# A decoder layer with an expert lookup: small tensors of gathered tokens by way of DRAM, transposes later, 96 gathered tokens instead of 88

## The chip, the core and the metric

The kernel runs on one core of a Trainium2 chip. The metric is the device time of one execution in microseconds (us). A profiled execution has a span (first to last instruction in the trace) and its own time, which also holds what lies around the span.

## What is computed

The input is 256 tokens of width 1024. The layer normalizes them, projects them, mixes them by linear attention in four heads and by block-sparse attention in eight, projects back and adds the input. Then comes the expert lookup, and that is where the change is:

```python
q = (xt @ w_query).reshape(T, 8, 2, 128)
s = einsum('thpk', q, subkeys)               # 8 heads, 2 halves, 128 sub-keys
sv, si = top_k(s, 16)                        # per half
cand = sv[:, :, 0, :, None] + sv[:, :, 1, None, :]
top_s, pos = top_k(cand, 16)                 # 16 of 256 candidates per head
expert = take(si[..., 0] * 128 + si[..., 1], pos);  gate = softmax(top_s)
act = gelu(einsum('thkd,td->thk', u_tab[expert], xt))
out = einsum('thk,thkd->td', gate * act, v_tab[expert])
```

Each token takes 8 x 16 = 128 of 16384 experts. The tables u and v hold 16384 rows of 1024 floats, 64 MB each.

## The kernel before

The tokens of the lookup are divided. For the first NS tokens the kernel gathers the 128 rows of u and of v that each needs. For the other ND = 256 - NS it multiplies with the whole of both tables and lets a grid of gates, zero where an expert was not chosen, pick the right ones.

**Dense part.** The tables pass through SBUF in tiles of 512 KB, 128 for u and 128 for v. SyncE's queue (SP) loads them in order into a ring of 14 buffers, the next load at every `take`. In the u stage (`for jp in range(64)`) each of the 128 tiles takes eight matmuls of 128x128 by ND columns (line 120); ScalarE applies the gelu (line 840). In the v stage each tile takes eight more (line 881), which add into three PSUM banks. At the end of the v stage DVE adds these to `x2d`, the residual (line 898), in three pieces, and they go out (line 899).

**Before the tables: the q stage.** 16 weight tiles for the queries are each divided into a high and a low part, by ScalarE (line 100) and DVE (line 101), and multiplied in three passes (lines 69 to 71); products with the sub-keys follow, each 128 columns wide (line 725). Between them DVE finds the 16 largest values; the rest of this search is a list `work[0]` for the first 128 tokens, worked off in the first nine pairs of tiles of the u stage, and a list `work[1]` for the other 128, spread up to pair `J0`. Its results (two index arrays `ij`, line 640, and the gates) are transposed on TensorE (`turn`, line 645, and `turn_gates`, line 684), spread by ScalarE (lines 647, 689), and from pair 31 on one-hot arrays and a grid of gates are made of them, four tokens at a time (lines 797 to 817).

**Gathered part.** I call one token's share of one table a "few". GpSimd (POOL) gathers the 128 rows of its experts in one indirect DMA of 512 KB into one of five buffers `rowsof` (line 743). For u, DVE multiplies the rows with the token's normalized row and sums along each row (line 751); for v, DVE multiplies each row by its gate times activation and adds to a running sum (lines 761, 763). `few_to` issues them evenly over both stages; they run u first, then v. The tokens share buffers by layout: FEW lists (first token, number of tokens n, parts m). In a layout, partitions are m blocks of n tokens, and block b handles slots b*128/m and up of each token. Then one column of indices names 128 rows and one DVE instruction handles them. `ys` holds a layout's n rows m times over (2, 8 and 16 blocks), `rs` their scales, `ixs` the expert numbers and `gs` the gates. ScalarE issues a DMA for each block and each of these four: `rows_of_few` (lines 568, 569) and `parts_of` (line 654), 4 x 26 = 104. At the end matmuls with the 0/1 matrix `sums` add the parts (line 892), DVE adds the residual (line 893), and the rows go out (line 894).

**What sets the order.** Each engine executes its instructions in one fixed order. The order in the program is set by a scheduler when the kernel is built: it simulates a timeline and hands each engine its instructions as they become ready there. Buffers and data dependencies turn into semaphore waits; an instruction that waits holds everything behind it on its engine.

Of the kernel before, what the change touches and what calls it, by code (L numbers as in the profile page):

```python
# [9 lines left out]
F32 = mybir.dt.float32  # L10
# [5 lines left out]
OP = mybir.AluOpType  # L16
AX = mybir.AxisListType

D = 1024
# [4 lines left out]
GS = 2.0 ** 14  # L24
NEXP = 128
J0 = 31
NS = 88
FEW = ((0, 64, 2), (64, 16, 8), (80, 8, 16))
ND = S - NS
SLOTS = 128  # L30
OFF = {"gq": 0, "gk": 256, "gv": 512, "gg": 1024, "gr": 1536, "mq": 1552, "mk": 2064, "mv": 2576}
# [4 lines left out]
def layer(ctx: ExitStack, tc: tile.TileContext, a):  # L36
    nc = tc.nc
    ve, sc_, pe, gp = nc.vector, nc.scalar, nc.tensor, nc.gpsimd
# [6 lines left out]
    keep = ctx.enter_context(tc.tile_pool(name="keep", bufs=1))  # L45

    def bank(tag):
        return psum.tile([128, 512], F32, name=tag, tag=tag, bufs=4 if tag == "sc" else 2)
# [3 lines left out]
    p = bank("mm")  # L52
# [158 lines left out]
    rows = {}  # L211
# [268 lines left out]
    x2T = mid.tile([128, NC, S], F32, name="x2T")  # L480
# [24 lines left out]
    act_p = ctx.enter_context(tc.tile_pool(name="actA", bufs=1))  # L505
# [6 lines left out]

    ixs = keep.tile([128, NS], U32, name="ixs")
    gs = keep.tile([128, NS], F32, name="gs")
    hs = keep.tile([128, NS], F32, name="hs")
    rs = keep.tile([128, 3], F32, name="rs")

    sums = act_p.tile([128, len(FEW), NS], F32, name="sums")
    gp.memset(sums, 0.0)
    for l, (t0, n, m) in enumerate(FEW):  # L520
        o = sums[:, l, t0:t0 + n]
# [3 lines left out]
    tk = tk_ctx.enter_context(tc.tile_pool(name="tk", bufs=1))  # L525
# [8 lines left out]
    rstd2 = tk.tile([128, NT], F32, name="rstd2")  # L534
    ss2 = tk.tile([128, NT, 2], F32, name="ss2")
    yf = wide.tile([128, NC, ND], F32, name="yf", tag="xhi")
    ys2 = wide.tile([128, 2, D], F32, name="ys", tag="xlo")
    ys = [ys2[:, 0], ys2[:, 1], act_p.tile([128, D], F32, name="ys3")]
    spillT = nc.dram_tensor("x2_cols", (128, NC, ND), F32, kind="Internal").ap()
    rows_x2 = nc.dram_tensor("x2_rows", (NS, D), F32, kind="Internal").ap()  # L540

    def x2_rows(tt):
        x2 = tk.tile([128, D], F32, name="x2")
        for hf in range(2):
            p = bank("tr")
            for c in range(4):
                pe.transpose(p[:, c * 128:(c + 1) * 128], x2T[:, 4 * hf + c, tt * 128:(tt + 1) * 128], ident)
            ve.tensor_copy(x2[:, hf * 512:(hf + 1) * 512], p)
            junk = tk.tile([128, 512], BF, name="junk", tag="junk")
            sc_.activation(junk, x2[:, hf * 512:(hf + 1) * 512], AF.Square, accum_out=ss2[:, tt, hf:hf + 1])  # L550
        if tt == 0:
            nc.scalar.dma_start(rows_x2, x2[0:NS])
        gp.tensor_tensor(rstd2[:, tt:tt + 1], ss2[:, tt, 0:1], ss2[:, tt, 1:2], op=OP.add)

    def norm2():
        nc.scalar.dma_start(spillT, x2T[:, :, NS:])
        rstd_of(rstd2, D, NT)
        row = as_row(tk, rstd2, "rrow2")
        for c in range(NC):
            ve.scalar_tensor_tensor(yf[:, c], x2T[:, c, NS:], n2[:, c:c + 1], row[:, NS:], op0=OP.mult, op1=OP.mult)  # L560

    def rows_of_few():

        n2b = tk.tile([128, D], F32, name="x2")
        nc.scalar.dma_start(n2b, a["n2b"])
        for l, (t0, n, m) in enumerate(FEW):
            for b in range(m):
                nc.scalar.dma_start(ys[l][b * n:(b + 1) * n], rows_x2[t0:t0 + n])  # L568
                nc.scalar.dma_start(rs[b * n:(b + 1) * n, l:l + 1], rstd2[t0:t0 + n, 0:1])  # L569
            ve.scalar_tensor_tensor(ys[l], ys[l], rs[:, l:l + 1], n2b, op0=OP.mult, op1=OP.mult)  # L570


    scs = [tk.tile([128, NT, 4, 128], F32, name=f"scs{b4}") for b4 in range(4)]
# [4 lines left out]
    ij = tk.tile([128, 2, NT, 8, 16], F16, name="ij")  # L578
    cands = [tk.tile([128, 8, 112], F32, name="cand") for _ in range(NT)]
    later = []  # L580

    def top16(vals, idx, src):
        ve.max(vals[:, 0:8], src)
# [51 lines left out]
    def slots3(tt, w, eq):  # L635
        n = 8
        while n > 1:
            ve.tensor_tensor(eq[:, :, 0:n], eq[:, :, 0:n], eq[:, :, n:2 * n], op=OP.add)
            n //= 2
        ve.tensor_tensor(ij[:, w, tt], eq[:, :, 0], eq[:, :, 1], op=OP.add)  # L640
        later.append(lambda: turn(tt, w))

    def turn(tt, w):
        p = bank("tr").bitcast(F16)
        pe.transpose(p[:, :128], ij[:, w, tt].rearrange("p h k -> p (h k)"), identh)
        src, ts = many(tt, p)
        sc_.copy(idxT[:, w, ts], src[:, :, None].to_broadcast([128, ts.stop - ts.start, 2]))

    def parts_of(dst, src):

        for t0, n, m in FEW:
            w = SLOTS // m
            for b in range(m):
                nc.scalar.dma_start(dst[b * n:(b + 1) * n, t0:t0 + w], src[t0:t0 + n, b * w:(b + 1) * w])  # L654

    def experts():

        num = tk.tile([128, SLOTS], U32, name="num")
        r, c = (ij[:, w, 0].rearrange("p h k -> p (h k)") for w in range(2))
        numf = tk.tile([128, SLOTS], F32, name="numf")  # L660
        ve.scalar_tensor_tensor(numf, c, 128.0, r, op0=OP.mult, op1=OP.add)
        ve.tensor_copy(num, numf)
        parts_of(ixs, num)

    def gates(tt):
        gt = top[:, tt]
# [5 lines left out]
    def gates2(tt):  # L672
        gt = top[:, tt]
        sm = tk.tile([128, 8], F32, name="sm")
        ve.tensor_reduce(sm, gt, AX.X, OP.add)
        ve.reciprocal(sm, sm)
        ve.tensor_tensor(gt, gt, sm[:, :, None].to_broadcast([128, 8, 16]), op=OP.mult)
        if tt == 0:
            parts_of(gs, gt.rearrange("p h k -> p (h k)"))
        later.append(lambda: turn_gates(tt))  # L680

    def turn_gates(tt):
        p = bank("tr")
        pe.transpose(p[:, :128], top[:, tt].rearrange("p h k -> p (h k)"), ident)

        src, ts = many(tt, p)
        full = tk.tile([128, 128], F32, name="full")[:, :ts.stop - ts.start]
        g16 = tk.tile([128, 128], F16, name="g16")[:, :ts.stop - ts.start]
        sc_.activation(full, src, AF.Copy, scale=GS)
        sc_.copy(g16, full)  # L690
        sc_.copy(gf[:, 0, ts], g16)
        ve.tensor_tensor(gf[:, 1, ts], full, g16, op=OP.subtract)


    work = [[(1.6, lambda b=b, tt=tt: top16(sv[:, tt, b], si[:, tt, b], scs[b // 4][:, tt, b % 4])) for b in range(16)]
            for tt in range(NT)]
# [48 lines left out]

    place = [l for l, (_, n, _) in enumerate(FEW) for _ in range(n)]

# [73 lines left out]
    left1 = sum(c for c, _ in work[1])  # L821
    all1, spent = left1, 0.0
    for jp in range(64):
        pv = bank("mm")[:, :2 * ND].rearrange("p (k t) -> p k t", k=2)
        turns, later = later, []
        for k in range(2):
            by_col_whole(pv[:, k], take(("u", jp), k), yf)
        for f in turns:
            f()
        if jp == J0:  # L830
            assert not work[1] and not later
            tk_ctx.close()
            actB_p = ctx.enter_context(tc.tile_pool(name="actB", bufs=1))
            act[1] = actB_p.tile([128, 64, ND], F32, name="actB")
            oh = ctx.enter_context(tc.tile_pool(name="oh", bufs=2))
            one_hots(0)
        o = act_at(2 * jp, 2 * jp + 2)
        T = 4 * done_q
        if T < ND:
            sc_.activation(o[:, :, T:], pv[:, :, T:], AF.Gelu)  # L840
        if T:
            gl = oh.tile([128, 2, ND], F32, name="gl", bufs=1)
            sc_.activation(gl[:, :, :T], pv[:, :, :T], AF.Gelu)
            ve.tensor_tensor(o[:, :, :T], o[:, :, :T], gl[:, :, :T], op=OP.mult)
        if work[0]:
            spent -= 4.8
            while work[0] and spent < 0:
                c, f = work[0].pop(0)
                spent += c
                f()  # L850
            j1 = jp + 1
        else:
            few_to((jp - j1 + 1) * 2 * NS // (64 - j1 + 61))
            while work[1] and all1 - left1 < all1 * (jp + 1 - j1) / (J0 - 1 - j1):
                c, f = work[1].pop(0)
                left1 -= c
                f()
        while jp > J0 and done_q < NQ and done_q * (62 - J0) < (jp - J0) * NQ:
            grid_group(done_q, 2 * jp + 2)
            done_q += 1  # L860
            if done_q % 2 == 1 and done_q + 1 < NQ:
                one_hots(done_q + 1)
# [3 lines left out]
    for _ in range(3):  # L866
        p = bank("sc")[:, :3 * ND]
# [6 lines left out]
    for jp in range(64):  # L874
# [13 lines left out]
        if jp == 62:  # L888
            for hf in range(2):
                fs = slice(hf * 512, (hf + 1) * 512)  # L890
                for l in range(len(FEW)):
                    pe.matmul(end[hf][0:NS], sums[:, l], ys[l][:, fs], start=l == 0, stop=l == len(FEW) - 1)  # L892
# [76 lines left out]
```

## Time and profile before

| | |
|---|---|
| three runs | 874.48, 874.9, 876.65 us |
| median | 874.9 us |
| profiled execution, own time | 877.12 us |
| its span | 875.3 us |
| TensorE matmuls (PE) | 823.0 us busy (94%) |
| TensorE weight loads (PEld) | 777.0 us (89%) |
| DVE | 482.1 us (55%) |
| ScalarE (ACT) | 247.3 us (28%) |
| GpSimd (POOL) | 215.1 us (25%) |
| DMA | 261.67 MB, 299 GB/s on average |

The table rows of u and v that are streamed and those that are gathered account for nearly all of the DMA bytes: 162.87 MB went through SP's queue and 92.29 MB through GpSimd's. Busy shares are averages over stages that differ; a matmul that has been issued and is being fed counts as busy. A record of line 881 or 120 is one matmul of 168 columns.

### The profile page before, as it was taken

To read this page: it belongs to the slowest core of one execution; us is meant where nothing else is said; L and a number is where in the kernel's file an instruction comes from. 1 tells how busy PE (TensorE), PEld (TensorE's weight loads), DVE (VectorE), ACT (ScalarE), POOL (GpSimd) and SP (SyncE) were. 2 spreads that over 40 slices of the span, in tenths; PEclk is the share of its full clock that TensorE was granted. 3 is DMA by queue.
4 is the path that set the end of the run, shared out by engine and by line. 5 is a ranking of instruction groups with operands and counts; after the bars stand their busy time and mean duration, and the time that the engine had idled before them with its cause. 6 is when DMAs were issued, how large, how long until landed. Compare 5 with 4: busy or idle time off the path is not lost.

```text
span 875.3 us, 14841 instructions
## 1 busy us (share of the span) xinstructions
PE 823.0 (94%) x5734; PEld 777.0 (89%) x5734; DVE 482.1 (55%) x1060; ACT 247.3 (28%) x660; POOL 215.1 (25%) x252
## 2 busy tenths in 40 slices
PE   9999999928997499999999999999999999999995
PEld 6876689828997399999999999999999999999993
DVE  4795367494899644446666777645455445410003
ACT  5556345403220211019677776200000000000000
POOL 4141103000001833323222232433333333300000
PEclk9997899967999699999999999999999999999998
DMA  9453027814976899999999999999999999999701
GB/s 340 167 167 121 25 79 229 248 45 139 328 236 222 301 403 409 408 409 408 400 339 360 367 352 382 349 408 408 409 409 408 409 408 409 409 409 354 234 2 48
DMA packets 75551, 261.67 MB, mean 299 GB/s; under 512 B 10433, under 2 KB 12497, under 8 KB 75353
## 3 DMA queue, kind: packets, MB, share of 16 engines
q1 hardware_dynamic: 44883, 162.87, 50.0%
q0 software_dynamic: 25344, 92.29, 27.4%
q10 hardware_dynamic: 5254, 5.57, 2.3%
q8 instruction: 45, 0.74, 0.3%
q14 instruction: 25, 0.20, 0.1%
HBM read 258.50 MB, written 2.10 MB: 298 GB/s over the span
## 4 chain that ended last, share of the span: by engine, by line
PE 82%; DVE 7%; DMA 5%; ACTq 3%; ACT 1%; issue 1%; POOL 1%; SPq 0%; DVEq 0%
PE sc L881 31%; PE mm L120 28%; PE mm L71 4%; PE mm L69 4%; PE mm L70 4%; DMA raw<-in_v_rows 2%; PE tr L808 2%; ACTq L654 1%; PE sc L388 1%; ACTq L569 1%; PE mm L892 1%; ACTq L568 1%; DMA xT<-in_xT 1%; DMA ixs<-num 1%; PE sc L369 1%
## 5 line engine op out<-in xcount | busy, mean ns | idle before, releaser
L120 PE MATMUL mm<-yf,raw 128*128 128x168 f32 x1184 | 175.8, 307 | 0.0
L120 PEld LDWEIGHTS mm<-yf,raw 128*128 128x128 f32 x1184 | 169.5, 190 | 0.4 <-DMA raw<-in_u 0.4
L761 DVE SCALAR_TENSOR_TENSOR ys<-rowsof,hs,ys 128x1024 f32<-128x1024 f32 x85 | 109.1, 1284 | 101.6 <-DMA rowsof<-in_v_rows,ixs 101.4
L743 POOL DMA_INDIRECT rowsof<-in_u_rows,ixs x88 | 93.5, 1062 | 276.5 <-DVE hs L751 152.6
L751 DVE CUSTOM_DVE_ANT_0 junkd<-rowsof,ys 128x1024 bf16<-128x1024 f32 x88 | 107.5, 1222 | 48.8 <-DMA rowsof<-in_u_rows,ixs 47.9
L743 POOL DMA_INDIRECT rowsof<-in_v_rows,ixs x88 | 84.8, 964 | 147.2 <-DVE ys L761 125.7
L797 ACT ACTIVATE B<-E,gf 128x128 f16<-128x128 f16 x336 | 102.1, 388 | 22.3 <-PE tr L808 16.3
L881 PEld LDWEIGHTS sc<-actB,raw 128*128 128x128 f32 x608 | 87.1, 190 | 3.2 <-DMA raw<-in_v_rows 2.2
L881 PE MATMUL sc<-actB,raw 128*128 128x168 f32 x608 | 89.8, 307 | 0.1
L101 DVE TENSOR_TENSOR lo<-raw,hi 128x1024 fp32r<-128x1024 f32 x48 | 58.9, 1233 | 47.4 <-ACT hi L100 47.4
L881 PE MATMUL sc<-actA,raw 128*128 128x168 f32 x576 | 82.9, 306 | 0.0
L881 PEld LDWEIGHTS sc<-actA,raw 128*128 128x128 f32 x576 | 82.3, 190 | 0.0
L100 ACT ACTIVATE hi<-raw 128x1024 fp32r<-128x1024 f32 x48 | 50.4, 1057 | 67.2 <-PE mm L71 21.8
L120 PEld LDWEIGHTS mm<-yf,hi 128*128 128x128 f32 x432 | 63.3, 193 | 3.1 <-ACT actA L840 3.1
L120 PE MATMUL mm<-yf,hi 128*128 128x168 f32 x432 | 65.9, 311 | 0.1
L120 PE MATMUL mm<-yf,lo 128*128 128x168 f32 x432 | 64.8, 307 | 0.0
L120 PEld LDWEIGHTS mm<-yf,lo 128*128 128x128 f32 x432 | 62.1, 190 | 0.0
L69 PE MATMUL mm<-qhi,hi 128*128 128x256 f32 x128 | 38.7, 303 | 15.1 <-ACT hi L100 15.0
L898 DVE TENSOR_TENSOR x2d<-x2d,sc 128x504 f32<-128x504 f32 (+1 forms) x3 | 1.9, 619 | 91.1 <-PE sc L881 91.1
L840 ACT ACTIVATE actA<-mm 128x336 f32<-128x336 f32 x32 | 14.3, 450 | 105.3 <-PE mm L120 85.7
L71 PE MATMUL mm<-qhi,lo 128*128 128x256 f32 x128 | 38.6, 304 | 4.7 <-DVE lo L101 4.7
L69 PEld LDWEIGHTS mm<-qhi,hi 128*128 128x128 f32 x128 | 26.6, 208 | 15.6 <-ACT hi L100 15.6
(266 smaller groups left out, 1181.6 us busy)
## 6 DMA issues: line engine op xcount, KB each, us to landing
raw<-in_u SPq DMA_DIRECT2D x74, 512.0 KB
raw<-in_v_rows SPq DMA_DIRECT2D x74, 512.0 KB
hi<-in_u SPq DMA_DIRECT2D x27, 512.0 KB
lo<-in_u SPq DMA_DIRECT2D x27, 512.0 KB
hi<-in_v_rows SPq DMA_DIRECT2D x27, 512.0 KB
lo<-in_v_rows SPq DMA_DIRECT2D x27, 512.0 KB
raw<-in_w_rows SPq DMA_DIRECT2D x20, 512.0 KB
raw<-in_w_q SPq DMA_DIRECT2D x16, 512.0 KB
```

Of the source, the lines that this page charges most:

```text
L69: pe.matmul(ps, sh, mh, start=first, stop=False)
L70: pe.matmul(ps, sh, ml, start=False, stop=False)
L71: pe.matmul(ps, sl, mh, start=False, stop=last)
L100: sc_.activation(hi, raw, AF.Copy)
L101: ve.tensor_tensor(lo, raw, hi.bitcast(F32), op=OP.subtract)
L120: pe.matmul(ps, rv[:, c], mov[:, c], start=(c == 0), stop=(c == NC - 1))
L743: gp.indirect_dma_start(g, None, a[name], bass.IndirectOffsetOnAxis(ap=ixs[:, k:k + 1], axis=0))
L751: ve.tensor_tensor_reduce(junk, g, ys[place[k]], 1.0, 0.0, OP.mult, OP.add, hs[:, k:k + 1])
L761: ve.scalar_tensor_tensor(sumS, g, hs[:, k:k + 1], sumS, op0=OP.mult, op1=OP.add)
L797: sc_.activation(B[:, k], E[:, k], AF.Copy, scale=gf[:, m, 4 * q + k:4 * q + k + 1])
L808: pe.matmul(pv[:, k], A[:, k], B[m][:, k], start=(m == 0), stop=(m == 1))
L881: pe.matmul(acc[c // 3][:, c % 3], raw[:, c * 128:(c + 1) * 128], act[j // 64][:, j % 64], start=False, stop=j == NEXP - 1 and c in (2, 5, 7))
```

## The change

NS goes from 88 to 96 and ND from 168 to 160. The gathered tokens stand in two layouts, 64 tokens in 2 parts and 32 in 4, instead of three; the third `ys` tile is gone, and so is the tile `rs`.

The rows of the gathered tokens are scaled and weighted where they stand, in one DVE instruction on 96 partitions, and `to_parts` then writes them to DRAM and reads each layout back with one DMA, whose source repeats the rows m times. Gates and expert numbers go the same way, with the slots divided into m parts. These nine DMAs are issued by GpSimd; ScalarE issues none of them. Three other DMAs (`rows_x2`, `spillT`, `n2b`) move from ScalarE's queue to SP's.

The transposes of indices and gates are no longer issued with the next pair of tiles but at the third pair after that in which their input was made (`at + 3`). The list `work[1]` is spread to end three pairs sooner.

```diff
-NS = 88
-FEW = ((0, 64, 2), (64, 16, 8), (80, 8, 16))
+NS = 96
+FEW = ((0, 64, 2), (64, 32, 4))
...
-            nc.scalar.dma_start(rows_x2, x2[0:NS])
+            nc.sync.dma_start(rows_x2, x2[0:NS])
...
-        nc.scalar.dma_start(spillT, x2T[:, :, NS:])
+        nc.sync.dma_start(spillT, x2T[:, :, NS:])
...
+    def to_parts(dst, name, src, cols):
+
+        there = nc.dram_tensor(name, (NS, src.shape[1]), src.dtype, kind="Internal").ap()
+        gp.dma_start(there, src)
+        for l, (t0, n, m) in enumerate(FEW):
+            rows = there[t0:t0 + n]
+            if cols:
+                rows = rows.rearrange("t (m w) -> m t w", m=m)
+            else:
+                rows = rows[None].to_broadcast([m, n, src.shape[1]])
+            gp.dma_start(dst(l), rows)
...
     def rows_of_few():
 
         n2b = tk.tile([128, D], F32, name="x2")
-        nc.scalar.dma_start(n2b, a["n2b"])
-        for l, (t0, n, m) in enumerate(FEW):
-            for b in range(m):
-                nc.scalar.dma_start(ys[l][b * n:(b + 1) * n], rows_x2[t0:t0 + n])
-                nc.scalar.dma_start(rs[b * n:(b + 1) * n, l:l + 1], rstd2[t0:t0 + n, 0:1])
-            ve.scalar_tensor_tensor(ys[l], ys[l], rs[:, l:l + 1], n2b, op0=OP.mult, op1=OP.mult)
+        nc.sync.dma_start(n2b, a["n2b"])
+        yrow = xrow
+        ve.scalar_tensor_tensor(yrow[0:NS], xrow[0:NS], rstd2[0:NS, 0:1], n2b[0:NS], op0=OP.mult, op1=OP.mult)
+        to_parts(lambda l: ys[l], "y_rows", yrow[0:NS], False)
...
-        later.append(lambda: turn(tt, w))
+        later.append((at + 3, lambda: turn(tt, w)))
...
-        parts_of(ixs, num)
+        to_parts(by_part(ixs), "experts", num[0:NS], True)
...
-            parts_of(gs, gt.rearrange("p h k -> p (h k)"))
-        later.append(lambda: turn_gates(tt))
+            to_parts(by_part(gs), "gates", gt[0:NS].rearrange("p h k -> p (h k)"), True)
+        later.append((at + 3, lambda: turn_gates(tt)))
...
     for jp in range(64):
+        at = jp
...
-        turns, later = later, []
+        turns, later = [f for d, f in later if d <= jp], [x for x in later if x[0] > jp]
...
-            while work[1] and all1 - left1 < all1 * (jp + 1 - j1) / (J0 - 1 - j1):
+            while work[1] and all1 - left1 < all1 * (jp + 1 - j1) / (J0 - 4 - j1):
```

The program's order shows two places. First the end of DVE's queue before, in the v stage: `ys<-rowsof,hs,ys` is a few of v, `x2d<-x2d,sc` one of the three additions of the dense sums, which need the last matmul of the v stage.

```order
L761 SCALAR_TENSOR_TENSOR ys<-rowsof,hs,ys 128x1024 x60
L763 TENSOR_SCALAR ys<-rowsof,hs 128x1024
L761 SCALAR_TENSOR_TENSOR ys<-rowsof,hs,ys 128x1024 x15
L763 TENSOR_SCALAR ys_1440<-rowsof,hs 128x1024
L761 SCALAR_TENSOR_TENSOR ys_1440<-rowsof,hs,ys_1440 128x1024 x4
L898 TENSOR_TENSOR x2d<-x2d,sc 128x504 x2
L761 SCALAR_TENSOR_TENSOR ys_1440<-rowsof,hs,ys_1440 128x1024
L898 TENSOR_TENSOR x2d<-x2d,sc 128x336
L761 SCALAR_TENSOR_TENSOR ys_1440<-rowsof,hs,ys_1440 128x1024 x2
L893 TENSOR_TENSOR res<-res,mm 88x512 x2
```

The same end of DVE's queue after the change (line 769 is the former 761, line 771 the former 763, line 907 the former 898):

```order
L771 TENSOR_SCALAR ys<-rowsof,hs 128x1024
L769 SCALAR_TENSOR_TENSOR ys<-rowsof,hs,ys 128x1024 x42
L907 TENSOR_TENSOR x2d<-x2d,sc 128x480
L769 SCALAR_TENSOR_TENSOR ys<-rowsof,hs,ys 128x1024
L907 TENSOR_TENSOR x2d<-x2d,sc 128x480
L907 TENSOR_TENSOR x2d<-x2d,sc 128x320
L769 SCALAR_TENSOR_TENSOR ys<-rowsof,hs,ys 128x1024 x20
L771 TENSOR_SCALAR ys<-rowsof,hs 128x1024
L769 SCALAR_TENSOR_TENSOR ys<-rowsof,hs,ys 128x1024 x31
L902 TENSOR_TENSOR res<-res,mm 96x512 x2
```

Before, three fews stood behind the first addition; now 53 do, and it stands between the 43rd and the 44th few of v.

Second, TensorE's queue in the u stage before, around the first transposes of indices (`tr<-identh,ij`): `mm<-yf,...` are the dense matmuls of line 120.

```order
L120 MATMUL mm<-yf,raw 128x168 x20
L645 LDWEIGHTS ij
L645 MATMUL tr<-identh,ij 128x128
L120 MATMUL mm<-yf,raw 128x168 x20
L645 LDWEIGHTS ij
L645 MATMUL tr<-identh,ij 128x128
L684 MATMUL tr<-ident,top 128x128
```

And after the change, where line 660 is the former 645 and line 692 the former 684:

```order
L120 MATMUL mm<-yf,raw 128x160 x26
L660 LDWEIGHTS ij
L660 MATMUL tr<-identh,ij 128x128
L120 MATMUL mm<-yf,raw 128x160 x14
L120 MATMUL mm<-yf,hi 128x160 x16
L660 LDWEIGHTS ij
L660 MATMUL tr<-identh,ij 128x128
L120 MATMUL mm<-yf,hi 128x160 x8
L120 MATMUL mm<-yf,lo 128x160 x8
L692 MATMUL tr<-ident,top 128x128
```

Counted from the start of the u stage, the first of these transposes has 170 dense matmuls ahead of it instead of 140.

## Rows read from the trace of the kernel before

**Rows 1.** Stretches: start:end, us, busy us (count) by engine, PEclk, DMA share, GB/s

```profile
165.00:201.00 36.00, 15.62 (x101) 14.72 (x100) 27.24 (x141) 8.11 (x12) 0.00 (x0) 0.72 0.29 83
206.75:226.93 20.18, 20.18 (x169) 20.18 (x168) 12.27 (x54) 7.05 (x9) 0.00 (x0) 0.96 0.61 200
227.00:276.00 49.00, 48.35 (x340) 47.47 (x339) 45.84 (x254) 10.29 (x17) 0.00 (x0) 1.00 0.79 273
276.00:298.00 22.00, 5.07 (x33) 4.36 (x32) 16.58 (x25) 1.10 (x4) 14.21 (x10) 0.67 0.80 259
562.00:731.00 169.00, 169.00 (x1188) 169.00 (x1188) 84.13 (x67) 0.45 (x1) 63.32 (x67) 1.00 1.02 406
```

**Rows 2.** Lines 568 and 654: count, ns (least, median, most), first and last start

```profile
L568 ACTq DMA_DIRECT2D ys<-x_rows x26: 308/472/615, 158.6 to 197.6; - x26
...
L654 ACTq DMA_DIRECT2D ixs<-num x26: 537/632/675, 276.7 to 294.4; - x26
```

**Rows 3.** ACT's timeline: start us, us, instruction, [idle before it <- what ended it]

```profile
198.76 2.00 ACT L100 ACTIVATE hi<-raw 128x1024 fp32r<-128x1024 f32 x2 [12.77 <-DMA rs<-rstd]
...
297.13 0.20 ACT L689 ACTIVATE full<-tr 128x40 f32<-128x40 f32 x1 [18.92 <-DMA ixs<-num]
```

**Rows 4.** Waits of weight loads, 140 to 420: us in total, times, longest

```profile
PEld mm L69 <- ACT hi L100: 15.6, 2, 15.2
PEld L645 <- DVE ij L640: 15.4, 3, 13.6
```

**Rows 5.** The gathers alone, 640 to 720: us, POOL busy, PEclk, DMA, GB/s

```profile
640.00:720.00 80.00, 29.03 (x31) 1.00 1.03 409
```

**Rows 6.** The chain that ended last: start us, us, engine and line, records

```profile
218.14 0.89 PE sc L725 x8
...
227.21 3.42 PE mm L120 x24
...
562.12 173.50 PE sc L881 x1216
...
854.28 1.72 PE mm L892 x4
```

**Rows 7.** DVE's timeline, 264 to 305

```profile
269.03 0.22 DVE L640 TENSOR_TENSOR ij<-eq 128x128 f16<-128x128 f16 x1
...
287.38 1.23 DVE L751 CUSTOM_DVE_ANT_0 junkd<-rowsof,ys 128x1024 bf16<-128x1024 f32 x1 [3.10 <-DMA rowsof<-in_u_rows,ixs]
...
302.83 1.23 DVE L751 CUSTOM_DVE_ANT_0 junkd<-rowsof,ys 128x1024 bf16<-128x1024 f32 x1 [0.56 <-DMA rowsof<-in_u_rows,ixs]
```

**Rows 8.** DVE's timeline, 556 to 870

```profile
558.61 2.60 DVE L761 SCALAR_TENSOR_TENSOR ys<-rowsof,hs,ys 128x1024 f32<-128x1024 f32 x2
...
735.37 1.28 DVE L761 SCALAR_TENSOR_TENSOR ys<-rowsof,hs,ys 128x1024 f32<-128x1024 f32 x1 [1.28 <-DMA rowsof<-in_v_rows,ixs]
...
860.89 0.68 DVE L898 TENSOR_TENSOR x2d<-x2d,sc 128x504 f32<-128x504 f32 x1 [90.94 <-PE sc L881]
...
862.34 1.28 DVE L761 SCALAR_TENSOR_TENSOR ys<-rowsof,hs,ys 128x1024 f32<-128x1024 f32 x1
...
863.95 2.60 DVE L761 SCALAR_TENSOR_TENSOR ys<-rowsof,hs,ys 128x1024 f32<-128x1024 f32 x2
```

**Rows 9.** POOL's timeline, issues of gathers

```profile
281.05 2.02 POOL L743 DMA_INDIRECT rowsof<-in_u_rows,ixs  x1 [117.07 <-PE tr L645]
...
560.16 1.86 POOL L743 DMA_INDIRECT rowsof<-in_v_rows,ixs  x1 [3.35 <-DVE ys L761]
...
736.92 0.94 POOL L743 DMA_INDIRECT rowsof<-in_v_rows,ixs  x1 [1.63 <-DVE ys L761]
```

**Rows 10.** Timeline of all engines, 859.5 to 876

```profile
859.83 2.44 PE L881 MATMUL sc<-actB,raw 128*128 128x168 f32 x16
...
866.61 3.27 PE L892 MATMUL mm<-ys,sums 128*88 128x512 f32 x4 [4.33 <-DVE ys L761]
...
870.63 0.32 ACTq L894 DMA_DIRECT2D out<-res  x1
```

More of the change, by code (lines that the diff above doesn't have):

```diff
@@ L515, in layer @@
     hs = keep.tile([128, NS], F32, name="hs")
-    rs = keep.tile([128, 3], F32, name="rs")
     sums = act_p.tile([128, len(FEW), NS], F32, name="sums")
@@ L537, in layer @@
     ys2 = wide.tile([128, 2, D], F32, name="ys", tag="xlo")
-    ys = [ys2[:, 0], ys2[:, 1], act_p.tile([128, D], F32, name="ys3")]
+    ys = [ys2[:, 0], ys2[:, 1]]
     spillT = nc.dram_tensor("x2_cols", (128, NC, ND), F32, kind="Internal").ap()
     rows_x2 = nc.dram_tensor("x2_rows", (NS, D), F32, kind="Internal").ap()
+    xrow = tk.tile([128, D], F32, name="yrow")
     def x2_rows(tt):
-        x2 = tk.tile([128, D], F32, name="x2")
+        x2 = tk.tile([128, D], F32, name="x2") if tt else xrow
         for hf in range(2):
@@ L560, in norm2, with by_part @@
             ve.scalar_tensor_tensor(yf[:, c], x2T[:, c, NS:], n2[:, c:c + 1], row[:, NS:], op0=OP.mult, op1=OP.mult)
+    def to_parts(dst, name, src, cols):
[8 more added lines that the diff above has]
+            gp.dma_start(dst(l), rows)
+    def by_part(dst):
+        return lambda l: dst[:, FEW[l][0]:FEW[l][0] + FEW[l][1]]
     def rows_of_few():
         n2b = tk.tile([128, D], F32, name="x2")
-        nc.scalar.dma_start(n2b, a["n2b"])
-        for l, (t0, n, m) in enumerate(FEW):
-            for b in range(m):
-                nc.scalar.dma_start(ys[l][b * n:(b + 1) * n], rows_x2[t0:t0 + n])
-                nc.scalar.dma_start(rs[b * n:(b + 1) * n, l:l + 1], rstd2[t0:t0 + n, 0:1])
-            ve.scalar_tensor_tensor(ys[l], ys[l], rs[:, l:l + 1], n2b, op0=OP.mult, op1=OP.mult)
+        nc.sync.dma_start(n2b, a["n2b"])
+        yrow = xrow
+        ve.scalar_tensor_tensor(yrow[0:NS], xrow[0:NS], rstd2[0:NS, 0:1], n2b[0:NS], op0=OP.mult, op1=OP.mult)
+        to_parts(lambda l: ys[l], "y_rows", yrow[0:NS], False)
     scs = [tk.tile([128, NT, 4, 128], F32, name=f"scs{b4}") for b4 in range(4)]
@@ L580, in layer @@
     later = []
+    at = 0
     def top16(vals, idx, src):
@@ L647, in turn @@
         sc_.copy(idxT[:, w, ts], src[:, :, None].to_broadcast([128, ts.stop - ts.start, 2]))
[L649 to L654, printed above, removed]
     def experts():
```

## The prediction

> **What bounds the kernel now.** I read the stage table first, then the chain of waits, the queues behind the engines that are waited for, and last the order in which DVE will meet its instructions. In the table of stretches [rows 1] TensorE works 15.6 of 36 us from 165 to 201 and only 5.1 of 22 from 276 to 298, and the granted clock sinks to a mean of 0.72 and 0.67. In the other three rows it is busy to within 0.7 us at a clock of 0.96 or more, and in v, from 562 on, the DMA engines are full besides, at 406 GB/s.
>
> The two holes have one neighbour. ScalarE issues 104 small DMAs: 52 that place the copied rows and their scales, 52 that spread indices and gates, at a median of 0.47 to 0.63 us each (two of the four sets of 26 are in [rows 2]). Its next split of a weight tile starts at 198.76 and the evacuation of a transpose at 297.13, each behind a train of them [rows 3]. TensorE's weight loads waited 15.6 us for that split and 15.4 us for the indices that DVE makes (ij) [rows 4].
>
> Where both memory streams run, a gather is issued every 2.58 us (31 in 80 us) [rows 5]. Gathers and table tiles are both 512 KB, so 409 GB/s is 1.28 us for one and 2.56 for one of each: they share evenly. TensorE needs a tile every 16 records of 142.7 ns (173.50 us for 1216 [rows 6]) = 2.283 us, so the tiles lose ground in the 14-buffer ring. By stage: q to 227.0, where the first u records start, u 335.0 us to 562.0, where v's start [rows 6], v 300.3 to 862.3, tail 13.0 to 875.3.
>
> **The change, part by part.** The sum is made in the profiled execution (span 875.3, own time 877.1); the runs' median, 874.9, is 0.4 under the span, and I carry that over.
>
> *ScalarE's queue, q stage.* The undisturbed stretch 206.75 to 226.93 takes 20.2 us for six of the 16 weight tiles with their score products [rows 1]; 16 tiles are 53.8, the 16 transposes and the row of norms about 2 more: from 144.8 to 200.6. DVE now does its top-16 pieces between the splits instead of in the hole; its work from 161.5 (eleven splits of 1.23, some 73 pieces of about 0.22, 5 us else) ends near 198, so I add 1.4: u begins at 202, 25.0 earlier. Bounds 198 (no hole at all) and 209 (a third of the hole stays). SP now issues three of the moved transfers: one waits for ScalarE's second square, as its ScalarE issue did, and the five loaded tiles ahead cover it. On GpSimd nothing but the gathers stands behind the new waits.
>
> *Transposes.* The order puts 170 dense matmuls ahead of the first ij transpose instead of 140, and 200 ahead of the second. At 272 ns those are 46 and 54 us after u begins; DVE's ij ended at 269.3 and 275.1, that is 42 and 48 after it (the first is in [rows 7]). So both waits and the one behind ScalarE go: 16.9 us of idle in 276 to 298 and 0.6 before [rows 1]. Next in line is ScalarE waiting for the gate exponentials, some 1 us, inside the bound.
>
> *160 columns.* Both 2048-record stages go from 168 columns to 160. By proportion a record is 135.9 ns; the line through the 128-column record (0.89 us for 8, 111 ns [rows 6]) gives 136.4. I take 136.0: a tile 2.176 us, 128 tiles 278.5 instead of 292.2, so 13.7 per stage. Two of the 42 grid groups go too, 0.9. u stage: 335.0 - 13.7 - 17.5 - 0.9 = 303, v begins at 505.
>
> *Eight more tokens, 16 more gathers.* This decides. A gather needs one DVE instruction (a "few") and one of five buffers. DVE runs in order, and in the new order only 71 fews stand ahead of its last u-stage instruction (92 before), 68 more ahead of the first x2d addition, and 53 behind it (3 before). That addition waits for the last dense matmul: DVE waited 90.9 us for it in this trace, and three fews ran only afterwards [rows 8]. So in v 68 fews run, about 70 gathers or 179 us at 2.56. Before, 207 us of sharing brought 79.7 tiles (81 less the reload of x2d) while 88.7 were used: 9 came from the ring and 4.5 us was lost. Now 68.6 + 9 tiles last 169 us: 10 lost by this, 4.5 if the ring is fuller; I take 8. The matmuls at L892 leave the stage but for four records (two pieces of 1.72 us before, one in [rows 6]; 3.4 gone). v: 300.3 - 13.7 - 3.4 + 3.5 = 286.7, TensorE's dense work ends at 792 instead of 862.3.
>
> *The tail.* Behind that end stand three additions and 53 fews. The first five have landed data: with the additions they end some 7 us after the matmuls (1.28 and up to 0.68 each [rows 8]). The other 48 go round a loop over five buffers: a few ends, GpSimd starts 0.27 later (736.65 to 736.92), takes 0.94 [rows 8, 9], the rows are usable 4.31 later (issue done 283.07, first few 287.38 [rows 7, 9]), the few takes 1.28: 6.8 us for five, 1.36 each. That is the lower row. But an issue begun while a few runs took 1.86, until 0.81 after that few ended (issue at 560.16; the few ended at 561.21), and below 1.55 a round GpSimd always starts under the next few. The upper row is the only stretch of the trace with gathers alone: ten fews started from 287.38 to 302.83, 1.72 each [rows 7]. I take 1.57, where the loop stops catching itself: 48 x 1.57 = 75.4.
>
> The Trainium skill ("DMA: Bandwidth & Descriptors", "Anatomy of one DMA — SWDGE (gpsimd) path") fits a GpSimd DMA at 2.0 us plus bytes over 436 GB/s: an estimate from it is 3.2 us for these 512 KB. The trace has 4.31. By the page the loop is 1.14, under DVE's own 1.28.
>
> Behind the last few: three pieces of two matmul records wait in order, at 0.8 us a record (866.61, 3.27 for four [rows 10]) 5.1, the addition 0.7, the output 4.7 (issued at 870.6 [rows 10], span's end 875.3) and hand-overs: 10.7. Tail: 7 + 75.4 + 10.7 = 93.1 instead of 13.0.
>
> Sum: -25.0 - 32.0 - 13.6 + 80.1 = +9.5 on the span, 884.8; on the median 884.4. I predict **884 us**.
>
> **Rivals.**
> *DVE alone paces the tail.* If rows land soon enough, 48 fews take 1.30 each: 62.4, end 872. It decides below 1.37 a few, where the loss is nil. For it: the 4.31 was measured while ScalarE's small DMAs also ran. Against: 4.3 to 4.9 for all of the next gathers there. This is the other side, a gain of 3 us, and what the page's fit would give.
> *DVE isn't held.* If the fews weren't queued behind the x2d addition, 121 would follow v's start at 2.56: 310 us, end at 505 + 310 + 11 = 826. Against: the three fews and three additions of this trace ran exactly in the listed order.
> *The gather starts late.* Reading the rows back in 2 or 4 blocks may go through few DMA engines. If one engine carries a sixteenth of 409 GB/s, 256 KB is 10 us, and 64 short runs behind as many table packets some 19. Gathers would begin near 277 rather than 260; 26 fews at 2.56 must pass before DVE makes the first one-hots, which TensorE needs near 348: about 5 us lost, span 890. The 16 us of slack speak against more.
> The Trainium skill states such a confinement (same page, "Rules for kernel authors": an outermost dimension of c under 16 keeps a DMA to at most c engines). No transfer of this trace shows it.
> *160 columns are no cheaper* (the weight load sets the pace): 27 us back, span 912. Against: 111 ns at 128 columns [rows 6].
>
> **How the numbers follow.** My forecast 0.74, DVE-paced 0.12, late start 0.08, not held 0.03, no cheaper 0.03. The likeliest's own range is 874 to 897: dense end 784 to 799 and 1.45 to 1.68 a few. The whole range starts at the DVE-paced tail with an early dense end (866) and goes to 1.72 a few with a late one (901). A measurement of this kernel can tell about 0.3%, 2.6 us. Faster: 0.6 of the DVE-paced case, the "not held", and a twentieth of the forecast: 0.14. Same: 0.35 of DVE-paced and a twelfth of the forecast: 0.11. Slower 0.75.
>
> **What would show it.** Dense u matmuls begin near 202 with ScalarE never behind a DMA; no weight load waits 5 us for ij; 16 records of v take 2.18; DVE waits over 100 us for TensorE before x2d; after the last dense matmul 53 fews run for about 80 us with TensorE idle and POOL's issues at 1.2 to 1.8. I am wrong if the fews of the tail come under 1.4 apart, if dense work ends outside 780 to 804, or if fews run between the additions' wait and the end of v.

## The result, and the profile after

The changed kernel takes 885.4 us (median of four runs, 882.99 to 886.83); the kernel before takes 875.77 on the same chips. The ratio is 1.010, 95% interval 1.007 to 1.014. It is slower, by 1.0%, and the interval leaves out 1. The profiled execution took 884.13 us with a span of 882.4. By stage, in us of the profiled executions:

| stage | before | predicted | after |
|---|---|---|---|
| u begins at | 227.0 | 202 | 195.7 |
| u stage | 335.0 | 303 | 302.6 |
| v stage | 300.3 | 286.7 | 285.6 |
| dense work ends at | 862.3 | 792 | 783.8 |
| after it | 13.0 | 93.1 | 98.5 |

The dense work ends 78.5 us earlier, and 85.5 us come back behind it. First the stretches, with the columns of [rows 1]:

```profile
165.00:195.70 30.70, 30.70 (x265) 30.70 (x265) 30.70 (x156) 11.98 (x15) 1.50 (x2) 1.00 0.72 207
...
244.00:266.00 22.00, 22.00 (x165) 21.96 (x164) 12.63 (x21) 2.81 (x9) 8.02 (x9) 1.00 0.84 272
562.00:640.00 78.00, 78.00 (x576) 78.00 (x576) 38.91 (x31) 0.00 (x0) 28.18 (x30) 1.00 1.03 409
785.00:873.00 88.00, 3.70 (x4) 0.96 (x4) 65.76 (x53) 0.00 (x0) 62.78 (x48) 0.51 0.87 295
```

The two holes of [rows 1] are gone: TensorE is full from 165 to 195.7, and from 244 to 266, which lies as far behind the start of the u stage as 276 to 298 did before. The last row is the new piece: 88 us with 3.7 us of matmul, 53 fews on DVE and 48 gathers, the clock at its lower level. The waits of TensorE's weight loads from 140 to 420, which answer to [rows 4], are all that is left of 15.6 and 15.4:

```profile
PEld L660 <- DVE ij L655: 1.8, 1, 1.8
PEld mm L120 <- ACT actA L849: 0.5, 1, 0.5
```

And DVE's timeline at the end of the dense work, which answers to [rows 8]:

```profile
782.52 0.66 DVE L907 TENSOR_TENSOR x2d<-x2d,sc 128x480 f32<-128x480 f32 x1 [110.52 <-PE sc L890]
783.10 1.28 DVE L769 SCALAR_TENSOR_TENSOR ys<-rowsof,hs,ys 128x1024 f32<-128x1024 f32 x1
784.29 1.05 DVE L907 TENSOR_TENSOR x2d<-x2d,sc 128x480 f32<-128x480 f32 x2
785.25 6.56 DVE L769 SCALAR_TENSOR_TENSOR ys<-rowsof,hs,ys 128x1024 f32<-128x1024 f32 x5
792.30 1.28 DVE L769 SCALAR_TENSOR_TENSOR ys<-rowsof,hs,ys 128x1024 f32<-128x1024 f32 x1 [0.48 <-DMA rowsof<-in_v_rows,ixs]
...
804.34 1.28 DVE L769 SCALAR_TENSOR_TENSOR ys<-rowsof,hs,ys 128x1024 f32<-128x1024 f32 x1 [0.63 <-DMA rowsof<-in_v_rows,ixs]
...
872.42 1.28 DVE L769 SCALAR_TENSOR_TENSOR ys<-rowsof,hs,ys 128x1024 f32<-128x1024 f32 x1 [1.53 <-DMA rowsof<-in_v_rows,ixs]
```

DVE stood 110.5 us before the first addition, with landed rows behind it. Then 53 fews ran until 873.7: six without a wait, and in the rest DVE waited for rows 27 times, 21.2 us together. GpSimd's issues in that stretch, which answer to [rows 9], are 1.32 us long on average (1.95 at most), where nearly all of those in the v stage before had 0.94:

```profile
804.82 1.61 POOL L751 DMA_INDIRECT rowsof<-in_v_rows,ixs  x1 [0.31 <-issue]
806.74 1.69 POOL L751 DMA_INDIRECT rowsof<-in_v_rows,ixs  x1 [0.30 <-issue]
808.74 1.45 POOL L751 DMA_INDIRECT rowsof<-in_v_rows,ixs  x1 [0.30 <-issue]
810.49 1.02 POOL L751 DMA_INDIRECT rowsof<-in_v_rows,ixs  x1 [0.30 <-issue]
```

### The profile page after: what moved, and what is told of

Its sections match the earlier page's. It is cut to its first block, busy times and chain, and to the rows that moved or that the text cites. A ratio compares the mean times of both kernels' runs of the same rounds, so it can differ in the third digit from the quotient of the medians.

```text
span 882.4 us, 14702 instructions
## 1 busy us (share of the span) xinstructions
PE 782.9 (89%) x5714; PEld 740.6 (84%) x5714; DVE 495.9 (56%) x1076; ACT 241.5 (27%) x642; POOL 245.9 (28%) x257
## 4 chain that ended last, share of the span: by engine, by line
PE 41%; DMA 22%; issue 19%; DVE 11%; POOL 5%; ACT 1%; SPq 0%; POOLq 0%; DVEq 0%; ACTq 0%
PE mm L120 24%; DMA rowsof<-in_v_rows,ixs 16%; DMA rowsof<-in_u_rows,ixs 5%; POOL rowsof L751 4%; PE mm L69 3%; PE mm L70 3%; PE mm L71 3%; DVE ys L769 2%; PE tr L816 2%; DVE lo L101 1%; PE sc L388 1%; DVE si L602 1%; DVE si L599 1%; DVE scs L600 1%; DVE sv L601 1%
## 5 line engine op out<-in xcount | busy, mean ns | idle before, releaser
L120 PE MATMUL mm<-yf,raw 128*128 128x160 f32 x1184 | 167.1, 300 | 0.3 <-ACT actA L849 0.3
L751 POOL DMA_INDIRECT rowsof<-in_v_rows,ixs x96 | 108.2, 1127 | 209.2 <-DVE ys L769 187.6
L769 DVE SCALAR_TENSOR_TENSOR ys<-rowsof,hs,ys 128x1024 f32<-128x1024 f32 x94 | 120.8, 1285 | 77.8 <-DMA rowsof<-in_v_rows,ixs 76.7
L759 DVE CUSTOM_DVE_ANT_0 junkd<-rowsof,ys 128x1024 bf16<-128x1024 f32 x96 | 117.4, 1223 | 70.7 <-DMA rowsof<-in_u_rows,ixs 70.4
L890 PE MATMUL sc<-actB,raw 128*128 128x160 f32 x608 | 86.0, 301 | 2.2 <-DMA raw<-in_v_rows 1.2
L890 PE MATMUL sc<-actA,raw 128*128 128x160 f32 x576 | 79.1, 299 | 0.0
L890 PEld LDWEIGHTS sc<-actA,raw 128*128 128x128 f32 x576 | 78.5, 190 | 0.0
L907 DVE TENSOR_TENSOR x2d<-x2d,sc 128x480 f32<-128x480 f32 (+1 forms) x3 | 1.7, 594 | 110.5 <-PE sc L890 110.5
L120 PE MATMUL mm<-yf,hi 128*128 128x160 f32 x432 | 62.4, 301 | 0.0
L120 PE MATMUL mm<-yf,lo 128*128 128x160 f32 x432 | 61.4, 300 | 0.0
L849 ACT ACTIVATE actA<-mm 128x320 f32<-128x320 f32 x32 | 13.8, 436 | 99.9 <-PE mm L120 99.9
L70 PE MATMUL mm<-qlo,hi 128*128 128x256 f32 x128 | 36.1, 283 | 0.0
## 6 DMA issues: line engine op xcount, KB each, us to landing
lo<-in_v_rows SPq DMA_DIRECT2D x27, 512.0 KB, 10.7
```

The lines of the kernel that those rows point to most:

```text
L70: pe.matmul(ps, sh, ml, start=False, stop=False)
L120: pe.matmul(ps, rv[:, c], mov[:, c], start=(c == 0), stop=(c == NC - 1))
L751: gp.indirect_dma_start(g, None, a[name], bass.IndirectOffsetOnAxis(ap=ixs[:, k:k + 1], axis=0))
L759: ve.tensor_tensor_reduce(junk, g, ys[place[k]], 1.0, 0.0, OP.mult, OP.add, hs[:, k:k + 1])
L769: ve.scalar_tensor_tensor(sumS, g, hs[:, k:k + 1], sumS, op0=OP.mult, op1=OP.add)
L890: pe.matmul(acc[c // 3][:, c % 3], raw[:, c * 128:(c + 1) * 128], act[j // 64][:, j % 64], start=False, stop=j == NEXP - 1 and c in (2, 5, 7))
```

## The experiments

Each was timed beside the kernel before on the same chip, whose median was 875.77 us in the first four and 876.34 in the other four.

**Additions behind all fews.** The additions read a number that DVE writes after the last few, so the order can't put them ahead.

```diff
+            one = gat.tile([128, 1], F32, name="one", bufs=1)
+            ve.tensor_scalar(one, ys[-1][:, 0:1], 0.0, 1.0, op0=OP.mult, op1=OP.add)
...
-        ve.tensor_tensor(x2d[:, cs], x2d[:, cs], acc[b][:, :cs.stop - cs.start], op=OP.add)
+        ve.scalar_tensor_tensor(x2d[:, cs], acc[b][:, :cs.stop - cs.start], one, x2d[:, cs], op0=OP.mult, op1=OP.add)
```

> The changed kernel, with the three x2d additions made to read a number that DVE writes after the last few, so that all 121 fews of the v stage stand ahead of them. Theory (DVE is held by the first addition): fews run through the whole v stage at 2.56 us each beside the table tiles, dense work ends some 8 us later than before the edit (near 793, tiles at 2.56 instead of 2.18), and what follows the last dense matmul shrinks from 98 us to 10 to 25; time 805 to 822 us. Rival (96 gathered tokens are simply too many for the gathers, wherever they stand in the order): fews again run for over 60 us after the last dense matmul, time above 860.

Measured: 818.6 us, ratio to before 0.933 (0.927 to 0.939). The v stage takes 304.0 us, dense work ends at 804.1, and 12.7 us follow. The theory holds, with 11 us more of dense time than I had put, since the tiles lose more beside 121 fews: TensorE's weight loads waited 23.1 us for table tiles in the v stage, against 6.7 in the changed kernel. Its stretches show it:

```profile
620.00:700.00 80.00, 76.87 (x523) 71.31 (x522) 39.81 (x31) 0.00 (x0) 28.53 (x31) 1.00 1.03 409
700.00:790.00 90.00, 84.96 (x559) 76.51 (x558) 44.42 (x35) 0.00 (x0) 33.27 (x36) 1.00 1.03 409
```

Gathers go on at one in 2.5 to 2.6 us, the DMA engines stay at 409 GB/s up to 790, and TensorE now waits for tiles. This version beats both kernels.

**88 tokens with the new path and the later transposes.**

```diff
-NS = 96
-FEW = ((0, 64, 2), (64, 32, 4))
+NS = 88
+FEW = ((0, 64, 2), (64, 16, 8), (80, 8, 16))
...
-    ys = [ys2[:, 0], ys2[:, 1]]
+    ys = [ys2[:, 0], ys2[:, 1], act_p.tile([128, D], F32, name="ys3")]
```

> The change without its token counts: NS 88 in the three layouts of before, 168 dense columns, but small tensors by way of DRAM and the later transposes. In its order 17 fews stand behind the first x2d addition. Theory (both holes of TensorE go with ScalarE's DMAs and the early transposes): u begins at 195 to 199 instead of 227, the u stage takes 316 to 320 us instead of 335, dense work ends near 813, and 17 fews with the end take some 37 us; time 842 to 858. Rival (the gain in u begins came from the 96-token layouts, not from the path): u begins after 210 and the time is above 862.

Measured: 852.5 us, ratio 0.971 (0.965 to 0.978). u begins at 197.3, the u stage takes 317.9, dense work ends at 814.6, 36.9 follow with 17 fews. Each number is inside what the theory said. Without the token counts the change is a gain, even with 17 fews held.

**96 tokens alone**, on the kernel before:

```diff
-NS = 88
-FEW = ((0, 64, 2), (64, 16, 8), (80, 8, 16))
+NS = 96
+FEW = ((0, 64, 2), (64, 32, 4))
```

> The kernel before with nothing but the token counts changed: 96 tokens in two layouts, 160 columns; 24 small DMAs on ScalarE's queue instead of 104, transposes as before; 53 fews behind the first addition. Theory (the holes are the number of small DMAs on ScalarE and the early ij transpose): with 12 of them the q stage ends at 203 to 210; the u stage keeps most of the wait for ij and takes 310 to 318 us; tail as in the changed kernel, 95 to 100; time 895 to 910. Rival (it is the round trip on ScalarE's queue that holds it, not the number): q stage ends near 225, time above 912. Rival (two layouts alone remove both holes): time within 884 to 890.

Measured: 894.8 us, ratio 1.020 (1.014 to 1.027). u begins at 204.4, the tail is 98.2: as the theory said, and the time falls just under its 895. But the u stage takes 302.5 us, not 310 to 318: with 12 DMAs in it instead of 52 its hole was gone. The transposes had not all stayed where they were, though: counted in the trace, the fourth ij transpose stands behind 480 dense matmuls here and behind 176 before, without any edit of that line. The q stage keeps a rest of its hole (columns of [rows 1]):

```profile
165.00:184.00 19.00, 14.41 (x108) 14.00 (x108) 15.98 (x56) 7.85 (x12) 0.00 (x0) 0.91 0.48 160
184.00:204.00 20.00, 20.00 (x173) 20.00 (x172) 20.00 (x106) 7.01 (x9) 0.00 (x0) 1.00 0.58 184
```

So the two layouts alone, with fewer DMAs on ScalarE, take away most of both holes, and the path by GpSimd takes 8.7 us more from the q stage. For the q stage that speaks for the number of DMAs; in the u stage the moved transpose may have its part.

**Seven gather buffers.**

```diff
-        g = gat.tile([128, D], F32, name="rowsof", tag="rowsof")
+        g = gat.tile([128, D], F32, name="rowsof", tag="rowsof", bufs=7)
```

(and so for `res`, which shares the buffers.)

> The changed kernel with seven gather buffers instead of five, all else and the ring of 14 as it was; 52 fews behind the first addition. Theory (the tail is a loop round the buffers: few, issue, landing, few; 8.5 us for five): the loop would be 1.21 a few, so DVE sets the pace: 1.28 to 1.40 a few, 16 to 20 us less tail; time 864 to 870. Rival (gathers alone move only some 305 GB/s, 1.70 us each, whatever is outstanding): pace 1.6 to 1.72, time 880 to 886. Between them (GpSimd's issues, held by each few, set it): 1.45 to 1.55, time 872 to 878.

Measured: 872.6 us, ratio 0.997 (0.994 to 1.000); tail 81.9 instead of 98.5, 52 fews at 1.41 us on average, most of them 1.32 apart. The pace falls between the first case and the third, the time into the third. The rival of a fixed 1.70 a gather is out. Of the 16.6 us that the tail lost, 12.3 reach the span, since the dense work ended at 788.2, later than in the changed kernel (783.8); no run shows why. Three issues and the stretch from 795 to 860:

```profile
800.15 1.01 POOL L751 DMA_INDIRECT rowsof<-in_v_rows,ixs  x1 [0.30 <-issue]
801.47 1.02 POOL L751 DMA_INDIRECT rowsof<-in_v_rows,ixs  x1 [0.30 <-issue]
802.79 1.01 POOL L751 DMA_INDIRECT rowsof<-in_v_rows,ixs  x1 [0.30 <-issue]
```

```profile
795.00:860.00 65.00, 3.70 (x4) 0.96 (x4) 58.20 (x47) 0.00 (x0) 44.91 (x42) 0.50 0.97 359
```

With enough rows on the way, DVE runs nearly without a gap (in the tail it waited for rows 5 times, 4.5 us together), and for most of it GpSimd issues once in each of its instructions, 1.32 us apart.

**The later transposes alone**, on the kernel before (all lines of the diff with `at` and `J0 - 4`):

```diff
-        later.append(lambda: turn(tt, w))
+        later.append((at + 3, lambda: turn(tt, w)))
```

> The kernel before (88 tokens, 104 small DMAs on ScalarE) with the later transposes alone, and the list of the second 128 tokens spread three pairs sooner. In its order the fourth ij transpose stands behind 432 dense matmuls instead of 176. Theory A (the idle time of TensorE at 276 to 298 is the wait for that fourth ij): u stage 317 to 321 us instead of 335, time 857 to 862. Theory B (it is ScalarE's train of DMAs, which also holds the gelus and with them TensorE's banks): u stage 330 to 336, time 870 to 877. q stage unchanged in both, u begins at 226 to 228.

Measured: 875.5 us, ratio 1.000 (0.997 to 1.002), u stage 334.4. Theory B. One thing was off: the u stage began at 222.0, not at 226 to 228, in a profiled execution of 870.6 us, the shortest of ten; the hole of the q stage is there as before. The weight loads' waits, and ScalarE's timeline around them:

```profile
PEld mm L120 <- ACT actA L842: 17.6, 1, 17.6
PEld mm L69 <- ACT hi L100: 15.6, 2, 15.1
```

```profile
271.69 17.76 ACTq L655 DMA_DIRECT2D ixs<-num  x26
289.49 1.30 ACTq L655 DMA_DIRECT2D gs<-top  x2
290.84 0.45 ACT L842 ACTIVATE actA<-mm 128x336 f32<-128x336 f32 x1 [23.87 <-DMA ixs<-num]
```

TensorE no longer waits for ij, but as long for a gelu that stands behind the train of DMAs. Taking away one of two waits that ran side by side had only uncovered the other. (In the trace the third ij transpose stands behind 432 dense matmuls and the fourth behind 464; both stood behind 176 before.)

**The new path alone** (88 tokens, transposes with the next pair as before):

```diff
-        later.append((at + 3, lambda: turn(tt, w)))
+        later.append(lambda: turn(tt, w))
```

> The kernel with 88 tokens and the small tensors by way of DRAM (the second experiment) without the later transposes; its first ij transposes stand behind 140 and 161 dense matmuls, as in the kernel before, but the fourth behind 448, because the order shifted. Theory (the path removes both holes, and the transposes' delay is worth only the few us by which the first one comes before its ij): u begins at 195 to 199, u stage 318 to 323, time 850 to 857. Rival (the delay is what removes the hole of the u stage): u stage 330 or more, time above 864.

Measured: 853.6 us, ratio 0.974 (0.971 to 0.977); u begins at 194.8, just ahead of what was expected, u stage 318.1. That agrees with the second experiment's 852.5 within its interval, so the lines that delay the transposes weren't needed. The late place itself isn't tested by this: the order put the third and fourth ij transposes behind 448 and 480 dense matmuls without those lines (counted in the trace). Only one wait of a weight load for ij is left:

```profile
PEld L660 <- DVE ij L655: 2.9, 1, 2.9
```

**A few of v in two halves:**

```diff
-            ve.scalar_tensor_tensor(sumS, g, hs[:, k:k + 1], sumS, op0=OP.mult, op1=OP.add)
+            for f in (slice(0, D // 2), slice(D // 2, D)):
+                ve.scalar_tensor_tensor(sumS[:, f], g[:, f], hs[:, k:k + 1], sumS[:, f], op0=OP.mult, op1=OP.add)
```

> The changed kernel with each few of v as two DVE instructions of 512 columns instead of one of 1024; order, buffers and bytes as in the changed kernel. Theory (an issue of GpSimd that begins under a DVE instruction lasts until 0.8 us after that one's end, and this lengthens the loop of the tail): no issue in the tail over 1.5 us instead of 1.95, the fews 1.45 to 1.62 apart instead of 1.73; time 874 to 881. Rival (the landing of the rows sets the pace, the long issues only follow): fews 1.70 to 1.80 apart, time 884 to 890.

Measured: 880.6 us, ratio 1.005 (1.003 to 1.007); 1.60 us a few against 1.72 in the changed kernel (both over all 52 gaps), the longest issue 1.46 instead of 1.95, the mean 1.11 instead of 1.32:

```profile
806.23 1.02 POOL L751 DMA_INDIRECT rowsof<-in_v_rows,ixs  x1 [0.30 <-issue]
807.56 1.46 POOL L751 DMA_INDIRECT rowsof<-in_v_rows,ixs  x1 [0.30 <-DMA rowsof<-in_v_rows,ixs]
809.33 0.94 POOL L751 DMA_INDIRECT rowsof<-in_v_rows,ixs  x1 [0.30 <-DMA rowsof<-in_v_rows,ixs]
```

So the length of DVE's instruction does set how long an issue is held, and that is part of the pace: the tail is 6.4 us shorter. (The span is only 3.7 us shorter, since the dense work ended at 786.6 here and at 783.8 in the changed kernel.) That the rest is the landing, which five buffers don't cover, fits the run with seven but isn't measured by itself.

**88 tokens, additions behind all fews** (the first and second edits together):

> The 88-token form of the change (second experiment) with the additions behind the last few, as in the first experiment. Theory (once DVE isn't held, TensorE bounds the 88-token form and the DMA engines the 96-token form): all fews end before the dense work, dense work ends at 812 to 816, time 822 to 829, so eight more gathered tokens are worth 4 to 10 us. Rival (the token counts make no difference once the order is mended): time within 817 to 820.

Measured: 826.6 us, ratio 0.942 (0.939 to 0.945); dense work ends at 818.5, some 3 us later than expected, and 8.5 us follow. The 96-token form took 818.6 beside runs of before that agree within 0.1%, so eight more gathered tokens are worth some 8 us once nothing is held. TensorE is the bound here: these are its last stretches, with DVE waiting 51.7 us for it and the DMA engines done.

```profile
700.00:790.00 90.00, 89.47 (x582) 83.12 (x583) 32.11 (x27) 0.00 (x0) 19.72 (x21) 1.00 1.03 406
790.00:818.00 28.00, 28.00 (x190) 26.95 (x190) 0.78 (x2) 0.00 (x0) 0.00 (x0) 1.00 0.06 18
```

## Why the prediction was right, step by step

**ScalarE's queue, q stage: mechanism right, size too small.** Forecast -25.0, measured -31.3, and 195.7 lies outside my bounds (198 to 209). The first of these matmuls ran at 142.4 instead of 144.8, which is 2.4 of the 6.3 us. From it to the last one it was 53.4 us, where I had put 53.8 for the tiles (from a row at a clock of 0.96), 2 for transposes and norms and 1.4 for DVE. In fact DVE was busy for all of 30.7 us from 165 on, and TensorE too: the search cost nothing there.

**Transposes: the sum right, the reason only in part, and a count wrong.** Forecast -32.0 for the u stage with the columns, measured -32.4. But I read 170 and 200 dense matmuls ahead of the first two transposes. Counted in the trace, where each of these matmuls is two records, there are 146 and 176, against 140 and 160; the number in the part on the change ahead of the prediction is wrong too. With 146 my own sum leaves the first transpose 2 us too early (39.7 against 42), and 1.8 is what it waited.

Nor were the first two the place that mattered: of the 15.4 us [rows 4] the fourth ij transpose alone waited 13.6. It stood behind 176 dense matmuls before and stands behind 464 after. Two things held TensorE there side by side, that ij and ScalarE's train of DMAs [rows 3]. The train is shown: with the transposes late in both, the u stage takes 334.4 us with it and 317.9 without it. What the late place is worth without the train stays open, since no run has the path and the fourth transpose behind 176. DVE finished that ij 72.1 us after the start of the u stage in the changed kernel and 61.5 after it in the run with the path alone. These are its lines, in that order:

```profile
267.59 0.22 DVE L655 TENSOR_TENSOR ij<-eq 128x128 f16<-128x128 f16 x1
```

```profile
256.06 0.22 DVE L655 TENSOR_TENSOR ij<-eq 128x128 f16<-128x128 f16 x1
```

176 dense matmuls take 48 us at 160 columns and 50 at 168. So an estimate from these numbers is that TensorE would have waited there for ij, for 11 us or more, without any train. The new order moved the transpose out of the way; the lines that delay it weren't needed for that.

**160 columns: right.** (A matmul is two records, so a tile has 16.) The chain after has 65.20 us for 480 records, 135.8 ns each; I took 136.0:

```profile
252.11 65.20 PE mm L120 x480
```

**Eight more tokens: right, and it decides.** 53 fews stood behind the first addition, DVE waited 110.5 us, the v stage took 285.6 against 286.7, and its weight loads waited 6.7 us for tiles, where I took 8. The first experiment shows that it is the place of the addition, not the number of fews: with the same 192 gathers the time is 818.6. I had priced "DVE isn't held" at 826; the additions' cost is then 67 us.

**The tail: mechanism right, its pace mis-sized.** The first five fews ended 6.7 us after the matmuls (7). The other 48 took 83.2 us, from 790.5 to 873.7, 1.73 each instead of 1.57, so 7.8 more. What came behind was 8.7 instead of 10.7: of my three pieces of matmul two were left, and one had run before. My choice between the rows failed: the upper row, 1.72, was the nearer situation (gathers alone, five buffers), and I argued it down to where "the loop stops catching itself". It didn't stop: 41 of the 48 issues of the tail began under an instruction of DVE. The halves show that this is part of the pace, and with seven buffers most fews came 1.32 apart.

By an estimate from the fit of the Trainium skill ("DMA: Bandwidth & Descriptors", "Anatomy of one DMA — SWDGE (gpsimd) path") DVE would have set the pace at about 1.30. Seven buffers come close to that (1.32 for most), five do not: the 872 by it was 13 us too low.

The total came nearer than the steps. On the span the terms are -31.3 - 32.4 - 14.7 + 85.5 = +7.1, against my +9.5; a q stage 6.3 us better and a tail 5.4 worse than forecast nearly cancel. That much of the closeness is luck.

**The rivals.** The gather didn't start late: the first one was issued at 256.62 and its few ran at 262.7.

```profile
256.62 1.08 POOL L751 DMA_INDIRECT rowsof<-in_u_rows,ixs  x1 [4.44 <-PE mm L120]
```

Columns are cheaper. "DVE paces the tail" is false for five buffers.

What stays open: how the pace of the tail divides between landing and held issues. A few in halves takes 1.41 us from its first start to its last end, against 1.28 in one piece, so the 0.11 us a few that halving saved is a lower bound for the second. Open too is what the late place of the transposes is worth beside the new path.

## What to carry to other kernels

When the order is fixed ahead, look in each in-order queue for the one instruction that waits for the end of a stage, and count what stands behind it; a single dependency that moves three additions turned a loss of 10 us into a gain of 57 here. A wait that a row names may be one of two that run side by side; taking it away then only uncovers the other. And an edit to one line can move instructions that it doesn't name, so count the order of every run again. Where the trace holds a stretch close to the situation that you forecast, take its number before a loop put together from parts.

## What the hardware showed

Gathers alone kept the DMA engines less productive than gathers mixed with table tiles: a share of 0.97 at 359 GB/s with seven buffers, against 1.03 at 409 in the v stage.

GpSimd's issue of a gather takes 0.94 us while DVE is idle, and up to 1.95 when it begins under an instruction of DVE of 1.28 us; with instructions of half the length it was at most 1.46. In the tail of the changed kernel 41 of 48 issues began under an instruction of DVE, and 40 of them ended 0.81 us after that instruction did (804.82 + 1.61 against 804.34 + 1.28); the other seven took 0.94.

The two reads of `y_rows` with 2 and 4 blocks outermost, 512 KB each, took 22.6 and 23.9 us to land, where the lines of the table tiles of 512 KB have medians of 7 to 12. The Trainium skill ("DMA: Bandwidth & Descriptors", "Rules for kernel authors") says that such an outermost dimension confines a DMA to so many engines; the slow landing agrees, though two and four blocks took nearly the same time. No run here tried another form, and it was off the path.
